# A list scheduler that orders the kernel: modulation weights may be loaded at any time, and dense products are drawn ahead of small ones when TensorE is counted as quiet

## The chip, the cores and the metric

One core of a Trainium2 chip runs the whole program. The metric is the time of one execution in device microseconds; less is better. Three runs of the kernel before took 2335.18, 2344.19 and 2348.64 us, so the median is 2344.19 us.

## What is computed

Two layers of a hybrid backbone over 512 latent and 256 context tokens, model width 1024. A layer is, cut to what matters here:

```python
sh_a, sc_a, gt_a, sh_m, sc_m, gt_m = ada_mod(cond, w_mod, b_mod)      # silu(cond) @ w_mod, 1024 x 6144
p = modulate(x, g_attn, sh_a, sc_a) @ w_in                            # one input projection
o_a = gdn_mixer(...)        # 8 heads of a gated delta rule, both directions, in chunks of 64 tokens
o_b = global_gqa(...)       # 4 query heads, all latent and context keys
o_c = window_gqa(...)       # 4 query heads, a band of keys and the context
x = x + gt_a * (concat(o_a, o_b, o_c) @ w_out)
x = x + gt_m * (square(relu(modulate(x, g_mlp, sh_m, sc_m) @ w1)) @ w2)
```

The context tokens go through the first layer in the same way. `ada_mod` depends on the conditioning alone, so its products can be made at any point before their results are used.

## The kernel before

**Work.** All products are split in a high and a low part and run as three passes. The input projection, the output projection and the MLP are dense: 128 rows by 128 columns of weights against 256 or 512 tokens. The delta rule is a chain over six pairs of token blocks ("units") and two groups of four heads: for each unit, `pre` builds and inverts the triangular blocks with many short operations of VectorE, GpSimd and 32x32 and 64x64 products, and `scan_step` carries the state forward with 64x64 and 128x64 products, whose PSUM tiles are called `pu`. The attention and all dense products use five PSUM banks called `ps`.

**Stages.** A layer has three phases. Phase 0 makes the input projection and the first group's chain, phase 1 the second group's chain, the attention and the modulation, phase 2 the output projection and the MLP. The program states the work in this order, but it isn't run in it.

**The order of the work.** `Program.layout` (L420) is a list scheduler that runs on the host while the kernel is built. It takes each operation's modelled duration from `cost` (L381), gives each a rank (the longest modelled path from it to the end of the program), and then steps through modelled time: on each of the four compute engines and on SyncE's queue, of the operations whose inputs are ready, the one with the highest rank goes next. The result is one fixed order of instructions for each engine. Nothing of it is decided on the chip, where each engine takes its instructions in that order and waits for its semaphores.

**Buffers.** A tile has a kind (L36 on) and takes one of that kind's slots when the first operation on it is placed (`room`, L494); an operation that finds no slot is set aside. Three kinds matter here. `sm` holds 512 KB of modulation weights and has two slots in phases 0 and 1. `st` holds the other weights, in three slots. `ps` is the PSUM kind, with five slots for everything dense.

**The modulation.** `mod_steps` makes a third `r` of the 6144 columns at a time: 16 loads of an `sm` tile, and from each tile four products of 32 rows by 256 columns, recorded as eight matmuls. All 64 products of one `r` add up in one `ps` tile, which is given back after the last of them. The first layer does `r` = 0 ahead of everything; `r` = 1, 2 and the next layer's `r` = 0 (48 loads) stand at the end of its phase 1. The second layer has `r` = 1 and 2 there (32 loads).

**The brake.** `AHEAD` (L50) and `HOARD` (L52) hold operations back (L545): an operation that needs a slot of a kind in `HOARD`, and whose rank is more than `AHEAD` of its engine behind the longest path still open, is laid aside until it comes within that distance. `AHEAD` is 1e5 ns for SyncE and practically endless for the others, so it is a brake on loads. `sm` is in `HOARD`, so the modulation loads are held back until 100 us of modelled path.

**TensorE's modelled clock.** The scheduler doubles a product's duration while it counts TensorE as cold. It keeps a sum of `dense` work in a running window; `dense` (`add`) is the share of the 128 rows that a product uses, times 0.6 if it has at most 64 columns. A modulation product, a weight product and a 128-row transpose count 1.0, the 64-row and 32-row products of the chain 0.15 to 0.5. The choice of the next operation does not look at that sum.

Of the kernel before, what the change touches and what calls it, by code (L numbers as in the profile page):

```python
# [48 lines left out]

AHEAD = (1e9, 1e9, 1e9, 1e9, 1e5)  # L50

HOARD = ("g", "sm", "t", "u", "a", "r", "kaq", "kv")  # L52

COPY = (0, 0, 0)
NU0 = 6
# [240 lines left out]
PE, ACT, DVE, POOL, SP = range(5)  # L296
# [3 lines left out]
WINDOW = 4096 / 1.2  # L300
COLD = 0.36
WARM = 0.66
TABLES = {AF.Exp: 0, AF.Tanh: 0, AF.Ln: 1}


class Program:
# [38 lines left out]
    def add(self, eng, name, args, kw):  # L345
# [30 lines left out]
        if eng == ACT:  # L376
            op.table = TABLES.get(args[2])
        self.ops.append(op)
# [41 lines left out]
    def layout(self):  # L420
        ops = self.ops
# [10 lines left out]
        for k, l in chains.items():  # L432
            n = KINDS[k][2] + KINDS[k][3] + max(KINDS[k][5:])
# [43 lines left out]
        clock, avail, future = [0.0] * 5, [[] for _ in range(5)], [[] for _ in range(5)]  # L477
        parked = {k: [] for k in KINDS}
        queues, front, order, table = 0.0, 0, [], 0
        warm, work, spill, window = False, 0.0, 0.0, 0  # L480
# [44 lines left out]
        while len(order) < len(ops):  # L525
            best = None
            for e in range(5):
                t = clock[e] if avail[e] else max(clock[e], future[e][0][0]) if future[e] else None
                if t is not None and (best is None or t < best[0]):
                    best = t, e  # L530
            if best is None and early:
                n = heapq.heappop(early)[1]
# [5 lines left out]
            t, e = best  # L538
            now = max(now, t)
            while future[e] and future[e][0][0] <= t:  # L540
                n = heapq.heappop(future[e])[1]
                heapq.heappush(avail[e], (-ops[n].rank, n))
            n = heapq.heappop(avail[e])[1]
            o = ops[n]
            if longest - o.rank > AHEAD[e] and n != front and n not in forced and any(  # L545
                    x.slot is None and x.kind in HOARD for x in o.tiles):
                heapq.heappush(early, (-o.rank, n))
# [10 lines left out]
            for x in o.tiles:  # L558
                if x.slot is None and x.kind in KINDS:
                    x.slot = got.pop(0)[1:]  # L560
                    r, i = x.slot
# [10 lines left out]
            if e == PE:  # L572

                w = int(t / WINDOW)
                while window < w:
                    warm = work > (COLD if warm else WARM) * WINDOW
                    work, window = spill, window + 1
# [3 lines left out]
                d = (end - t) * o.dense  # L581
                over = min(1.0, max(0.0, end - (w + 1) * WINDOW) / (end - t))
                work, spill = work + d * (1 - over), spill + d * over
# [16 lines left out]
            for x in o.tiles:  # L600
                if x.kind in KINDS:
                    x.left -= 1
                    x.end = max(x.end, end + 150)
                    if not x.left:
                        r, i = x.slot
# [14 lines left out]
            while early and (longest + early[0][0] <= AHEAD[ops[early[0][1]].eng] or early[0][1] == front):  # L620
                n = heapq.heappop(early)[1]
# [1161 lines left out]
```

## Time and profile before

| | |
|---|---|
| median of three runs | 2344.19 us |
| the profiled execution | 2342.02 us |
| its span | 2340.2 us |
| mean granted TensorE clock | 0.947 of full speed |
| matmul records on TensorE | 18792, busy 2143.4 us (92% of the span) |

The span is what the profiler's rows add up to; the execution's own time is 1.8 us longer. Times in rows are microseconds from the span's start. PE is TensorE (PEld its weight loads), DVE is VectorE, ACT is ScalarE, POOL is GpSimd, SPq is SyncE's queue, which issues all transfers. Nearly every instruction has the line L675, where the placed operations are issued, so rows are told apart by the names of the tiles: `ps<-sm,cs` is a modulation product, `ps<-b,w` a dense one, `pu<-...` one of the chain. Engines overlap, so busy times don't add up to the span.

### The profile page before, as it was taken

How to read it: one execution, taken by the hardware profiler on the slowest of the kernel's cores; microseconds unless marked ns; L12 is line 12 of the kernel's file. 1: busy time of each engine (PE TensorE's matmuls, PEld its weight loads, DVE VectorE, ACT ScalarE, POOL GpSimd, SP SyncE). 2: the span in 40 equal slices, each digit the busy share in tenths (PEclk: the TensorE clock that was granted, in tenths of full speed). 3: DMA queues.
4: the chain of work that ended last, by engine and by line, in shares of the span. 5: the costliest groups of instructions: out<-in, count | busy, mean ns of one | idle time of the engine just before them, and what ended most of it. 6: DMA issues, size and time to landing. Idle time of an engine off the chain costs nothing. (4 is left out here: it accounts for less than half of the span.)

```text
span 2340.2 us, 46868 instructions
## 1 busy us (share of the span) xinstructions
PE 2143.4 (92%) x18792; PEld 1688.3 (72%) x18792; DVE 1389.6 (59%) x3249; ACT 902.7 (39%) x1728; POOL 591.8 (25%) x1170
## 2 busy tenths in 40 slices
PE   5999998789978999999999898998769988999999
PEld 2787877456647788888888776688636666777777
DVE  4788677688764633333333487888876855334333
ACT  4756324455522521212122374543425544222321
POOL 0275435455440000000000025656763400000000
PEclk8999889799999999999999998999979989999999
DMA  7344323765453111221221224343574422223222
GB/s 277 96 133 123 108 83 96 220 177 166 143 160 116 53 57 64 70 72 46 73 72 59 95 80 121 96 134 110 155 208 138 151 73 84 87 90 105 94 90 81
DMA packets 170746, 260.63 MB, mean 111 GB/s; under 512 B 44448, under 2 KB 107424, under 8 KB 170528
## 3 DMA queue, kind: packets, MB, share of 16 engines
q1 hardware_dynamic: 170528, 257.64, 35.7%
q8 instruction: 147, 2.41, 0.4%
q14 instruction: 71, 0.58, 0.1%
HBM read 220.26 MB, written 37.32 MB: 110 GB/s over the span
## 5 line engine op out<-in xcount | busy, mean ns | idle before, releaser
L675 PE MATMUL ps<-b,w 128*128 128x512 f32 (+1 forms) x3936 | 848.1, 362 | 12.5 <-ACT b L675 6.7
L675 PEld LDWEIGHTS ps<-b,w 128*128 128x128 f32 x3936 | 655.4, 191 | 145.1 <-ACT b L675 10.1
L675 PE MATMUL ps<-h,w 128*128 128x512 f32 (+1 forms) x2304 | 480.8, 358 | 1.9 <-DVE w L675 0.9
L675 PEld LDWEIGHTS ps<-h,w 128*128 128x128 f32 x2304 | 381.6, 188 | 75.0 <-DVE w L675 4.9
L675 ACT ACTIVATE w<-st 128x1024 fp32r<-128x1024 f32 x192 | 197.9, 1054 | 572.9 <-PE ps L675 572.0
L675 DVE TENSOR_TENSOR w<-st,w 128x1024 fp32r<-128x1024 f32 x192 | 233.0, 1242 | 239.3 <-PE ps L675 163.1
L675 POOL TENSOR_TENSOR lb<-l,cst 128x72 fp32r<-128x72 f32 (+7 forms) x768 | 241.3, 350 | 62.4 <-ACT l L675 36.4
L675 DVE SCALAR_TENSOR_TENSOR x<-ps,mod,x 128x512 f32<-128x512 f32 (+1 forms) x120 | 77.2, 659 | 278.2 <-PE ps L675 278.0
L675 PE MATMUL ps<-w,b 128*128 128x256 f32 x1536 | 234.8, 298 | 4.8 <-DVE w L675 4.1
L675 ACT ACTIVATE g<-ps 128x512 f32<-128x512 f32 (+3 forms) x286 | 150.1, 540 | 199.4 <-PE ps L675 193.7
L675 PEld LDWEIGHTS ps<-w,b 128*128 128x128 f32 x1536 | 206.2, 197 | 14.4 <-DVE w L675 5.0
L675 POOL TENSOR_TENSOR g<-g 128x16 f32<-128x16 f32 x12 | 2.3, 225 | 720.5 <-ACT g L675 720.5
L675 DVE TENSOR_TENSOR q<-q,u 128x16 f32<-128x16 f32 (+4 forms) x360 | 131.3, 365 | 16.7 <-ACT u L675 10.6
L675 DVE TENSOR_TENSOR g<-g 128x512 f32<-128x512 f32 (+3 forms) x112 | 57.8, 541 | 120.6 <-ACT h L675 117.2
L675 ACT ACTIVATE u<-pu 128x384 f32<-128x384 f32 (+3 forms) x138 | 61.0, 449 | 150.1 <-PE pu L675 119.2
L675 DVE SCALAR_TENSOR_TENSOR g<-ps,par,g 128x511 f32<-128x511 f32 (+3 forms) x176 | 106.3, 618 | 7.8 <-ACT g L675 7.0
L675 PE MATMUL ps<-sm,cs 128*32 128x256 f32 x688 | 88.9, 445 | 19.5 <-DMA sm<-w_mod 14.0
L675 PE MATMUL ps<-cst,g 128*128 128x128 f32 (+1 forms) x502 | 90.3, 295 | 17.9 <-ACT g L675 11.3
L675 ACT ACTIVATE g<-ps,t 128x256 f32<-128x256 f32 (+2 forms) x144 | 75.3, 530 | 49.2 <-DVE t L675 41.8
L675 POOL TENSOR_TENSOR v<-u,gt 64x256 f32<-64x256 f32 x80 | 51.9, 649 | 148.0 <-DVE u L675 100.3
L675 PEld LDWEIGHTS ps<-cst,g 128*128 128x128 f32 (+1 forms) x502 | 59.3, 147 | 38.6 <-ACT g L675 21.6
L675 DVE TENSOR_TENSOR g<-g,g 128x512 f32<-128x512 f32 (+3 forms) x129 | 67.9, 546 | 29.1 <-ACT g L675 23.6
(138 smaller groups left out, 2665.8 us busy)
## 6 DMA issues: line engine op xcount, KB each, us to landing
st<-w SPq DMA_DIRECT2D x128, 512.0 KB, 4.3
sm<-w_mod SPq DMA_DIRECT2D x86, 512.0 KB, 4.7
st<-w_qkv SPq DMA_DIRECT2D x24, 512.0 KB, 4.4
st<-w_tm SPq DMA_DIRECT2D x24, 512.0 KB, 4.1
kv<-kv SPq DMA_DIRECT2D x96, 128.0 KB, 3.7
u<-gd SPq DMA_DIRECT2D x88, 128.0 KB, 3.5
kaq<-kq SPq DMA_DIRECT2D x80, 128.0 KB, 3.6
st<-w_out SPq DMA_DIRECT2D x16, 512.0 KB, 4.7
```

The lines of the kernel that those rows point to most:

```text
L675: getattr(engines[o.eng], o.name)(*[real(x) for x in o.args], **{k: real(x) for k, x in o.kw.items()})
```

## The change

`sm` leaves the list of kinds that are held back. And on TensorE, when the operation of highest rank is not dense (under 0.9), others are ready, and the modelled window has passed or its dense sum is behind (under half of the elapsed part while warm, under 0.8 of it while cold), then the ready dense operation of highest rank goes first, and the small one is put back.

```diff
-HOARD = ("g", "sm", "t", "u", "a", "r", "kaq", "kv")
+HOARD = ("g", "t", "u", "a", "r", "kaq", "kv")
...
+KEEP_WARM, GET_WARM, FULL = 0.5, 0.8, 0.9
...
             n = heapq.heappop(avail[e])[1]
+            if e == PE and ops[n].dense < FULL and avail[e]:
+
+                into = t - window * WINDOW
+                if t >= (window + 1) * WINDOW or work < (KEEP_WARM if warm else GET_WARM) * into:
+                    d = [x for x in avail[e] if ops[x[1]].dense >= FULL]
+                    if d:
+                        d = min(d)
+                        avail[e].remove(d)
+                        heapq.heapify(avail[e])
+                        heapq.heappush(avail[e], (-ops[n].rank, n))
+                        n = d[1]
             o = ops[n]
```

No operation is added, removed or resized. The instructions of each engine come in another order, and tiles take other slots.

## Rows read from the trace of the kernel before

**Rows 1.** The page's list of costly groups: TensorE's modulation products in the whole run.
```profile
L675 PE MATMUL ps<-sm,cs 128*32 128x256 f32 x688 | 88.9, 445 | 19.5 <-DMA sm<-w_mod 14.0 <-DVE cs L675 5.5
```

**Rows 2.** Windows by stage: length, busy us of each engine, PEclk, DMA share, GB/s.
```profile
60.00:240.00 180.00, 173.99 (x1589) 140.99 (x1589) 151.89 (x337) 115.34 (x186) 89.07 (x163) 1.00 0.42 120
240.00:400.00 160.00, 147.35 (x1783) 128.45 (x1784) 110.93 (x259) 56.56 (x111) 70.23 (x112) 0.90 0.29 87
400.00:500.00 100.00, 72.05 (x808) 44.43 (x808) 79.70 (x246) 37.73 (x105) 54.16 (x109) 0.74 0.76 218
500.00:640.00 140.00, 133.92 (x1918) 89.77 (x1919) 106.55 (x361) 77.85 (x222) 69.72 (x158) 0.98 0.48 147
640.00:712.00 72.00, 50.84 (x939) 32.33 (x938) 48.87 (x175) 19.30 (x47) 24.66 (x55) 0.87 0.48 147
...
1340.00:1640.00 300.00, 276.09 (x3161) 224.07 (x3160) 250.44 (x592) 155.90 (x265) 155.37 (x311) 0.94 0.38 107
1640.00:1760.00 120.00, 85.83 (x1228) 59.02 (x1227) 97.83 (x264) 34.90 (x78) 81.95 (x155) 0.83 0.64 182
1760.00:1880.00 120.00, 114.43 (x1680) 78.74 (x1680) 89.73 (x324) 65.29 (x185) 43.43 (x101) 0.97 0.43 134
```

**Rows 3.** The same stages, TensorE's modulation products alone: length, busy us, PEclk, DMA share.
```profile
400.00:500.00 100.00, 15.92 (x120) 0.74 0.76 218
500.00:640.00 140.00, 19.31 (x152) 0.98 0.48 147
640.00:712.00 72.00, 14.42 (x112) 0.87 0.48 147
...
1640.00:1760.00 120.00, 15.57 (x112) 0.83 0.64 182
1760.00:1880.00 120.00, 17.64 (x144) 0.97 0.43 134
```

**Rows 4.** Timeline of TensorE at the end of the first layer's phase 1.
```profile
659.03 0.65 PE L675 MATMUL pu<-s,u 32*32 32x32 f32 x32 [3.03 <-POOL s L675]
...
707.60 1.09 PE L675 MATMUL pu<-cst,u 128*128 128x128 f32 x4 [7.48 <-DVE u L675]
709.90 15.30 PE L675 MATMUL ps<-b,w 128*128 128x512 f32 x64 [1.21 <-ACT b L675]
```

**Rows 5.** Timeline of SyncE's queue: first modulation loads of phase 1, and a late run of them.
```profile
408.05 0.82 SPq L675 DMA_DIRECT2D sm<-w_mod  x2
...
662.70 23.92 SPq L675 DMA_DIRECT2D sm<-w_mod  x7
```

**Rows 6.** The chain that ended last, between 1735 and 1770 us.
```profile
1739.90 5.85 DMA sm<-w_mod
...
1747.93 6.24 DMA a<-kB
```

**Rows 7.** Windows of 20 us, all instructions, columns as in Rows 2.
```profile
240.00:260.00 20.00, 15.53 (x257) 10.84 (x258) 14.58 (x32) 10.99 (x20) 11.12 (x27) 0.74 0.15 50
...
320.00:340.00 20.00, 18.16 (x173) 14.94 (x171) 11.87 (x24) 6.09 (x14) 5.01 (x5) 0.80 0.45 137
340.00:360.00 20.00, 20.00 (x153) 18.63 (x153) 12.39 (x40) 5.12 (x10) 13.89 (x32) 0.83 0.30 87
1420.00:1440.00 20.00, 16.94 (x271) 14.54 (x270) 16.49 (x33) 5.81 (x12) 11.28 (x30) 0.82 0.37 111
1440.00:1460.00 20.00, 18.24 (x157) 14.29 (x158) 14.45 (x40) 5.19 (x10) 8.89 (x16) 0.83 0.27 76
```

**Rows 8.** Two of these windows, TensorE's products with weights alone, columns as in Rows 3.
```profile
240.00:260.00 20.00, 5.73 (x24) 0.74 0.15 50
...
340.00:360.00 20.00, 17.96 (x113) 0.83 0.30 87
```

**Rows 9.** Waits of the whole run: TensorE for VectorE to read out a bank.
```profile
PE ps L675 <- DVE g L675: 17.6, 9, 4.2
```

**Rows 10.** Window of 20 us in the first layer's input projection, columns as in Rows 2.
```profile
120.00:140.00 20.00, 20.00 (x162) 17.14 (x162) 15.41 (x27) 11.32 (x19) 11.05 (x21) 1.00 0.83 242
```

## The prediction

> **What bounds the kernel now.** I read first what the edit can touch, the modulation products: 688 records, 88.9 us of TensorE in the run [rows 1]. The table of stages then says where TensorE is short of time and where it isn't [rows 2]. Phase 0 of the first layer (60 to 400 us) keeps it busy for 321.3 of 340 us. Then come 400 to 500 us with 72.05 of 100, 500 to 640 with 133.92 of 140, and the end of phase 1, 640 to 712, with 50.84 of 72. The second layer repeats this: 276.09 of 300 us, then 85.83 of 120, then 114.43 of 120. So in each layer TensorE is full, then starved, then full again, and the first layer ends starved. The same stages with the modulation products alone show what the brake does: none before 400 us, 15.92 us in the starved stage, 19.31 us in the full one, 14.42 us at the end; in the second layer 15.57 and then 17.64 us in the full stage [rows 3]. The first of these loads after the opening goes out at 408 us [rows 5], though nothing but the brake keeps it from 60 us on. The timeline of the first layer's end shows small products waiting 3.03 us for GpSimd and 7.48 us for VectorE: there the delta-rule chain sets the end, and the modulation fills holes [rows 4]. The chain of waits has one more place: a modulation load of 5.85 us, and right behind it the attention's keys, 6.24 us [rows 6].
>
> **The brake off, first layer.** Nothing is added; work moves. The 48 loads may go from 60 us on, and their products have the lowest rank, so they run where the plan sees TensorE free or where the new rule prefers them.
>
> (a) The 19.31 us in the full stage 500 to 640 leave it. TensorE is 96% busy there, so I count all of it: -19.3 us (bounds 0, if the chain sets the pace there too, and -19.3).
>
> (b) The 14.42 us at the end leave too. TensorE is free for 21.2 of 72 us, so the cover is the chain's latency: -2 us (bounds 0 and -14.4).
>
> (c) Those 33.7 us go ahead of 500 us. TensorE is free there for 6.0 + 12.7 + 28.0 = 46.6 us [rows 2], but in holes of a few us, and the plan fills only holes that it foresees; a product put in a full stretch pushes what is behind it. Bounds 0 and +33.7; between them no row decides, so I take half, +16.9.
>
> Sum of the first layer: -4.4 us.
>
> **The brake off, second layer.** (d) 17.64 us leave 1760 to 1880, where TensorE is 95% busy: -17.6 us (bounds 0 and -17.6). (e) They go ahead of 1760, where 23.9 + 34.2 = 58.1 us are free, more than three times as much; again half, +8.8 (bounds 0 and +17.6). (f) The load in the chain of waits is gone from its place by then: -6 us, the 5.85 of that landing (bounds 0, and -12.1 if the keys behind it also land at once). Sum: -14.8 us.
>
> What queues behind what: SyncE issues in one order. Earlier, an `sm` load waits there for the products that read its slot before; behind it stand weight loads, stores of keys and queries, and the units' inputs, for which TensorE and GpSimd wait. In a late stretch seven such loads took 23.92 us of the queue's time [rows 5]. I count nothing for this, since the plan puts a load only after the slot's modelled end; the price, if that cover is gone, is a rival below.
>
> The stretch 120 to 140 us has the transfers at 0.83 and 242 GB/s [rows 10], so a load of 512 KB there costs the weight load behind it about 512 KB / 242 GB/s = 2.2 us. The Trainium skill says (DMA: Bandwidth & Descriptors, section "Issuing engines are not separate DMA queues") that all transfers of a core end on the same 16 engines and interleave there, which speaks against moving loads into that stretch; by it ten loads in the 40 us around it would cost up to 22 us, where TensorE has no slack. I take 0, since TensorE is full there and the slots of `sm` come free slowly.
>
> **Dense ahead of small.** (g) Gain. The granted clock is 0.90 over 240 to 400 and 0.94 over 1340 to 1640 [rows 2]; full speed throughout would give back 0.10 x 160 + 0.06 x 300 = 34 us, the bound on one side, with 0 on the other. But 340 to 360 us lies at 0.83 with 17.96 of 20 us in weight products [rows 7, 8]: dense work was already there. In 240 to 260 (clock 0.74, weights only 5.73 us), 320 to 340 (0.80), 1420 to 1440 (0.82) and 1440 to 1460 (0.83) there is something to mix; these lost 5.2 + 4.0 + 3.6 + 3.4 = 16.2 us. I take half, -8. The starved stages have lower clocks still (0.74 and 0.83), but what TensorE lacks there is ready work, and the modulation that filled them is partly spent earlier, so I count no gain from them.
>
> (h) Cost. Each swap makes a small product of the chain, and all behind it in the queue, wait for a dense one: 15.30 us / 64 = 0.24 us by the run of 128x512 products [rows 4]. The trace doesn't show how many swaps there are. If they fill half of the time at the low clock (2 x 34 = 68 us) and all of it lies on the chain, they cost 34 us; if dense work is ready anyway and the order merely changes, nothing. TensorE is full in those stages, so the order there costs little: +4.
>
> **Sum.** -4.4 - 14.8 - 8 + 4 = -23.2 us against the profiled execution's 2342.0, so 2318.8. The median lies 2.2 us above that execution, so I forecast 2321 us, with a range of its own of 2304 to 2332.
>
> **Rivals.** *All holes absorb.* If (c) and (e) are 0, because enough foreseen holes lie ahead, the sum is -19.3 - 2 - 17.6 - 6 - 8 + 4 = -49, or 2295 us. For it: 105 us are free ahead of the full stages for 51 us of work. Against: the holes of phase 0 are short. Chance 0.15.
>
> *The work moves and nothing ends sooner.* If the plan sees no holes that the chip has, (c) is +33.7 and (e) +17.6: -19.3 - 2 + 33.7 - 17.6 + 17.6 - 6 - 8 + 4 = +2, so about 2346 us. For it: phase 0 is full, and the first layer's end is the chain's, not TensorE's. This is also the case in which the change doesn't do what it says, as when the loads go early and their products keep their rank's late place. Chance 0.23.
>
> *A bank is missing (slower).* All 64 products of one third add up in one of the five `ps` banks. Started early and fed drop by drop, that third holds a bank through most of phase 0, where the projection's slices need banks while VectorE reads them out. The nearest price: nine waits of TensorE for VectorE's read-out sum to 17.6 us, so 1.96 us each, with five banks [rows 9]. If each of the 24 slices of the two layers waits so once more, that is +47, and with -23 the time is 2368 us. It decides from (23 + 12) / 24 = 1.5 us for each slice. Against it: the attention, in the full stages, then has that bank back. Chance 0.14. The Trainium skill (Perfetto Trace Analysis, section "Matmul Optimizations") asks that all PSUM banks be used, and a bank parked for a sum in waiting goes against it; the trace so far bears it out only with nine short waits.
>
> *SyncE's queue is held (slower).* If seven early loads hold the queue as the late ones did, 23.92 us each layer, units and weights come late: +48 - 23 = +25, or 2369 us. Against it: in that late stretch little else had to be issued. Chance 0.08.
>
> **How the numbers follow.** Forecast 0.40. Half a per cent, 11.7 us, is about what a measurement of this kernel can tell from no change (its three runs span 13.5 us). Faster by more: 0.40 + 0.15 = 0.55. Same: 0.23. Slower: 0.14 + 0.08 = 0.22. Both signs have weight, so the range reaches beyond the forecast's own: down to 2285, which holds the absorbed case with 10 us below it, and up to 2362, which holds the unmoved case and the smaller half of the slower ones. Left out are some 0.05 below and 0.13 above.
>
> **What would show it.** Right: modulation products from 60 to 400 us and from 1340 to 1640, few or none after 500 and 1760; the stages 500 to 640 and 1760 to 1880 shorter by 15 us or more; attention loads no longer behind modulation loads; a clock above 0.90 and 0.94 in phase 0. Wrong: the attention starting later by as much as its stage is shorter (the moved work was pushed, not absorbed); TensorE waiting for VectorE or ScalarE before `ps` products in phase 0 (the bank); SyncE waiting for `ps` products ahead of weight loads (the queue); or a longer stretch of small products in the starved stages, with a lower clock, since their filler is gone.

## The result, and the profile after

The changed kernel takes 2369.9 us (median of four runs, 2360.5 to 2371.7), beside 2342.6 us for the kernel before in the same session: a ratio of 1.011, 95% interval 1.007 to 1.015. It is slower by 27 us, where 2321 us and a gain were forecast, and above the range. The profiled execution took 2370.42 us, with a span of 2368.6 us.

Before the stages, the span is best split in two: the time in which TensorE was busy, and the rest. The page's list of engines, after:

```profile
PE 2183.9 (92%) x18792; PEld 1713.3 (72%) x18792; DVE 1390.9 (59%) x3249; ACT 904.1 (38%) x1728; POOL 600.4 (25%) x1170
```

Busy time of PE rose from 2143.4 to 2183.9 us, by 40.5 us, for the same 18792 products. The rest of the span fell from 2340.2 - 2143.4 = 196.8 to 184.7 us, by 12.1. The difference of the spans, 28.4 us, is +40.5 - 12.1: TensorE doesn't wait longer, its products take longer. The mean clock is the same, 0.947 in both. By the trace's record of the clock, TensorE was busy at the lower level (1.2 GHz) for 184.8 us before and 198.8 us after; if busy time there counts half, that is an estimated 7 us of the 40.5, and 33.5 us are left.

The windows up to the first layer's residual sum, and from there to the second layer's, before (columns as in [rows 2]):

```profile
0.00:722.90 722.90, 623.04 (x7272) 459.65 (x7273) 532.69 (x1447) 339.24 (x728) 308.18 (x601) 0.91 0.49 150
722.90:1929.90 1207.00, 1123.53 (x9853) 917.11 (x9852) 692.57 (x1607) 445.13 (x848) 283.63 (x569) 0.95 0.32 96
```

and after:

```profile
0.00:749.60 749.60, 639.94 (x7287) 474.02 (x7288) 535.38 (x1447) 338.24 (x727) 303.58 (x601) 0.91 0.47 145
749.60:1956.90 1207.30, 1145.73 (x9839) 926.76 (x9839) 691.40 (x1607) 447.58 (x849) 296.78 (x569) 0.96 0.31 95
```

The first part is longer by 26.7 us (PE busy +16.9, idle +9.8), the second by 0.3 (busy +22.2, idle -21.9). In both TensorE does about the same products in more time.

The stages of [rows 2], after. A stage here covers other work than before, since everything comes later:

```profile
60.00:240.00 180.00, 168.06 (x1536) 130.53 (x1536) 134.01 (x291) 105.54 (x171) 80.81 (x161) 0.99 0.50 144
240.00:400.00 160.00, 149.24 (x1678) 128.84 (x1676) 118.78 (x281) 58.27 (x105) 68.94 (x110) 0.98 0.31 95
400.00:500.00 100.00, 75.59 (x979) 50.05 (x979) 77.39 (x233) 39.30 (x101) 49.35 (x98) 0.80 0.69 200
500.00:640.00 140.00, 128.72 (x1677) 88.60 (x1676) 108.23 (x356) 71.17 (x201) 68.58 (x139) 0.94 0.49 149
640.00:712.00 72.00, 56.60 (x1039) 41.84 (x1039) 53.44 (x194) 26.45 (x79) 32.68 (x84) 0.82 0.16 49
```

Between 240 and 400 us the granted clock is 0.98, against 0.90 before: most of the low-clock time of [rows 7] is gone. TensorE was busy 1.9 us longer there and made 1678 products against 1783. The counts alone say little, since these are other products: by shape, 818 of 128x128 against 751, but 276 of 64x64 against 360 and 512 of 32x32 against 576. The same work in more time shows only in the whole run.

The modulation products alone, after (columns as in [rows 3]):

```profile
60.00:240.00 180.00, 7.21 (x88) 0.99 0.50 144
240.00:400.00 160.00, 2.48 (x8) 0.98 0.31 95
400.00:500.00 100.00, 16.15 (x128) 0.80 0.69 200
500.00:640.00 140.00, 18.08 (x129) 0.94 0.49 149
640.00:712.00 72.00, 0.00 (x0) 0.82 0.16 49
...
1340.00:1640.00 300.00, 1.68 (x16) 0.95 0.38 109
1640.00:1760.00 120.00, 16.65 (x104) 0.89 0.61 181
1760.00:1880.00 120.00, 20.07 (x128) 0.88 0.45 141
```

The full stages kept them: 18.08 us against 19.31, and 20.07 against 17.64. What went early (9.7 us before 400) came out of the first layer's end, where 14.42 us became none.

What TensorE does with its time is in its timeline. In the changed kernel, where 64 products `pu<-s,s` of 32x32 are next in the chain and dense `ps<-w,b` are ready:

```profile
261.78 0.31 PE L688 MATMUL pu<-s,s 32*32 32x32 f32 x10
262.01 0.38 PE L688 MATMUL ps<-w,b 128*128 128x256 f32 x1
262.33 0.32 PE L688 MATMUL pu<-s,s 32*32 32x32 f32 x12
262.57 0.38 PE L688 MATMUL ps<-w,b 128*128 128x256 f32 x1
262.88 0.31 PE L688 MATMUL pu<-s,s 32*32 32x32 f32 x10
263.12 0.38 PE L688 MATMUL ps<-w,b 128*128 128x256 f32 x1
263.43 0.31 PE L688 MATMUL pu<-s,s 32*32 32x32 f32 x12
263.68 0.50 PE L688 MATMUL ps<-w,b 128*128 128x256 f32 x2
264.11 0.38 PE L688 MATMUL pu<-s,s 32*32 32x32 f32 x20
264.42 1.56 PE L688 MATMUL ps<-w,b 128*128 128x256 f32 x11
```

The rule of the change has broken one run of small products into five, with one or two dense products in each gap. From the first start to 264.42 that is 2.64 us for 64 small and 5 dense products. The same kinds in unbroken runs, in the timeline of the experiment e5_runs:

```profile
287.12 4.30 PE L685 MATMUL ps<-w,b 128*128 128x256 f32 x34
291.35 0.75 PE L685 MATMUL pu<-s,s 32*32 32x32 f32 x64
292.03 2.85 PE L685 MATMUL ps<-w,b 128*128 128x256 f32 x22
```

Here 64 small ones take 0.68 us (291.35 to 292.03), and a dense one 4.23 / 34 = 0.124 us. That makes 0.68 + 5 x 0.124 = 1.30 us. The broken order costs 1.34 us more, for eight more changes between the two shapes: 0.17 us each. The granted clock is 1.00 in both stretches, and TensorE is busy all the time, so no list of waits shows it.

### The profile page after: what moved, and what is told of

Same layout as the page of the kernel before. It is cut to its first block, busy times and chain, and to the rows that moved or that the text cites. A ratio compares the mean times of both kernels' runs of the same rounds, so it can differ in the third digit from the quotient of the medians.

```text
span 2368.6 us, 46878 instructions
## 1 busy us (share of the span) xinstructions
PE 2183.9 (92%) x18792; PEld 1713.3 (72%) x18792; DVE 1390.9 (59%) x3249; ACT 904.1 (38%) x1728; POOL 600.4 (25%) x1170
## 4 chain that ended last, share of the span: by engine, by line
PE 66%; DVE 10%; POOL 2%; issue 2%; ACT 2%; DMA 1%; SPq 0%; ACTq 0%; DVEq 0%; POOLq 0%
PE ps L688 58%; PE pu L688 8%; DVE q L688 3%; DVE t L688 2%; DVE g L688 1%; POOL lb L688 1%; DVE u L688 1%; ACT g L688 1%; DVE w L688 1%; DVE kaq L688 0%; POOL g L688 0%; DMA sm<-w_mod 0%; DVE v L688 0%; ACT w L688 0%; ACT u L688 0%
## 5 line engine op out<-in xcount | busy, mean ns | idle before, releaser
L688 POOL TENSOR_TENSOR lb<-l,cst 128x72 fp32r<-128x72 f32 (+7 forms) x768 | 246.2, 355 | 85.7 <-ACT l L688 47.9
L688 PE MATMUL ps<-w,b 128*128 128x256 f32 x1536 | 241.4, 297 | 4.1 <-DVE w L688 3.5
L688 ACT ACTIVATE g<-ps 128x512 f32<-128x512 f32 (+4 forms) x286 | 149.9, 540 | 215.3 <-PE ps L688 212.5
L688 DVE TENSOR_TENSOR q<-q,u 128x16 f32<-128x16 f32 (+4 forms) x360 | 141.5, 393 | 16.0 <-ACT u L688 10.0
L688 PE MATMUL ps<-sm,cs 128*32 128x256 f32 x688 | 94.4, 452 | 21.7 <-DMA sm<-w_mod 16.0
L688 DVE SCALAR_TENSOR_TENSOR g<-ps,par,g 128x510 f32<-128x510 f32 (+3 forms) x176 | 106.2, 617 | 7.4 <-ACT g L688 6.6
L688 ACT ACTIVATE u<-pu 64x256 f32<-64x256 f32 (+3 forms) x138 | 61.3, 449 | 125.5 <-PE pu L688 99.5
L688 PE MATMUL pu<-u,kaq 64*64 64x64 f32 (+1 forms) x1344 | 84.1, 241 | 5.7 <-DVE u L688 4.1
```

The source lines that it names most:

```text
L688: getattr(engines[o.eng], o.name)(*[real(x) for x in o.args], **{k: real(x) for k, x in o.kw.items()})
```

## The experiments

Four theories were set against each other. **A:** the early modulation products push the rest, and the first layer's end lacks its filler. **B:** a dense product drawn ahead delays the chain. **C:** any new order differs by some 10 us or more, whatever made it. **D:** each time TensorE leaves small products for dense ones and comes back costs it about 0.23 us (0.20 to 0.235 by the starts of neighbouring products without idle time between them), and the change adds round trips. The expectation of e4_unbroken counts some 106 of them; the schedulers' orders have 431 runs of small products before and 526 after, which is 95 more, and in the traces the runs of products that use fewer than 128 rows number 415 and 504. Where an expectation gives the runs of a kernel not yet on the chip, they are counted in the order that its scheduler wrote.

A finer count was made once all had run, and it stands in the table: how often the part of the array that a product uses (the first figure in the timeline's rows, 32\*32, 64\*64, 128\*64, 128\*128 ...) is another than that of the product before it. Busy time and the rest of the span are those of the profiled execution, which is not the median: in e10 and e12 it took 2381.1 and 2325.3 us, 11 and 12 us more.

| kernel | changes of shape | PE busy, us | span less busy | median, us | ratio (95%) |
|---|---|---|---|---|---|
| before | 1172 | 2143.4 | 196.8 | 2342.6 | |
| after | 1372 | 2183.9 | 184.7 | 2369.9 | 1.011 (1.007-1.015) |
| e1_loads_only | 1166 | 2155.0 | 219.2 | 2377.6 | 1.016 (1.013-1.019) |
| e2_mix_only | 1417 | 2198.6 | 195.3 | 2399.8 | 1.025 (1.022-1.029) |
| e3_placebo | 1190 | 2145.0 | 201.6 | 2348.1 | 1.004 (1.002-1.005) |
| e4_unbroken | 1184 | 2139.5 | 189.6 | 2335.8 | 1.000 (0.997-1.003) |
| e5_runs | 1004 | 2098.3 | 203.6 | 2304.4 | 0.987 (0.984-0.989) |
| e6_many_runs | 2806 | 2683.5 | 215.8 | 2901.0 | one run |
| e7_runs_loads | 1013 | 2110.1 | 187.9 | 2296.5 | 0.982 (0.980-0.985) |
| e8_loads_placebo | 1190 | 2157.0 | 185.6 | 2341.1 | 1.001 (0.999-1.003) |
| e9_both | 998 | 2096.6 | 206.7 | 2304.1 | 0.986 (0.984-0.988) |
| e10_after_placebo | 1347 | 2186.0 | 193.1 | 2370.4 | 1.013 (1.010-1.017) |
| e11_mix_placebo | 1376 | 2182.0 | 184.4 | 2368.6 | 1.012 (1.008-1.015) |
| e12_best_placebo | 1022 | 2116.8 | 206.7 | 2313.2 | 0.989 (0.986-0.993) |

Each ratio is to runs of the kernel before beside it on the same chip (their medians lie between 2337.2 and 2342.6 us).

### Each half alone, and neither

**e1_loads_only:** only `sm` is taken off the brake.

```diff
-HOARD = ("g", "sm", "t", "u", "a", "r", "kaq", "kv")
+HOARD = ("g", "t", "u", "a", "r", "kaq", "kv")
```

> The brake on the modulation loads is taken off, the choice of dense products is left as before. Theory A (the early products push a full TensorE, and the end of the first layer's phase 1 runs at the low clock for want of filler): this part alone makes nearly all of the change, 2360 to 2372 us, with the first scan output of the first layer 8 to 15 us later than before (174 us) and a granted clock under 0.7 in the last 50 us of phase 1. Theory B (the swaps of dense ahead of small products delay the chain): 2335 to 2350 us, the loss is in the other part. Theory C (the order is reshuffled and any order differs by some 10 us): no relation to the parts; the gains and losses of the two parts don't add up to the whole.

**e2_mix_only:** only the rule that draws dense products ahead, as in the change; `sm` stays on the brake.

> Dense products are drawn ahead of small ones, the modulation loads stay held back. Theory A: 2330 to 2348 us, no loss; the end of the first layer's phase 1 keeps its modulation products and a granted clock over 0.85. Theory B: 2360 to 2372 us, with the scan outputs of the first layer later by 15 us or more. Theory C: anything between 2325 and 2365.

**e3_placebo:** neither; GpSimd's modelled cost is 2 ns higher, which alone shuffles the order.

```diff
-            return 148 + (1.667 if op.name != "tensor_tensor" or n < 400 else 2.0) * n, 0
+            return 150 + (1.667 if op.name != "tensor_tensor" or n < 400 else 2.0) * n, 0
```

> Neither part: the kernel before, with the scheduler's modelled cost of a GpSimd operation raised from 148 to 150 ns, which changes the order in places that have nothing to do with the change. Theories A and B: within 10 us of the kernel before. Theory C: as far away as the change, 15 us or more in either direction.

Both halves lost, by 1.6 and 2.5%, and each more than the two together; the shuffle lost 0.4%. So the parts don't add up, and a loss of e1's size had to be tried in another order before it could be blamed on the loads (e8). Neither theory A nor B had these times: 2377.6 us lies above A's range for e1, and 2399.8 above all ranges for e2. The shuffle is smaller than theory C wanted (15 us). The two lose in different places. e2 has TensorE busy for 55 us more. e1 has 11.6 us more of that and 22.4 us more of the rest: it stands still in the second layer, where the chain of waits of e1_loads_only reads

```profile
1724.62 4.38 DMA qC<-r
...
1737.11 4.00 DMA sm<-w_mod
1741.16 1.12 PE ps L675 x8
1742.72 4.59 DMA kC<-r
...
1750.24 5.95 DMA a<-kB
```

The collision of [rows 6], a modulation load and then the attention's keys, is still there, with the stores of queries and keys around it.

### The change without its broken runs

**e4_unbroken:** the changed kernel, but a dense product is drawn ahead only where the product before it was dense. The rule may put off a run; it can't break into one.

```diff
...
-            if e == PE and ops[n].dense < FULL and avail[e]:
+            if e == PE and ops[n].dense < FULL and avail[e] and full:
...
+                full = o.dense >= FULL
```

> The changed kernel, but a dense product is drawn ahead of a small one only where the product before was dense too, so a run of small products is never broken; the order then has 419 runs of small products in place of 526. Theory D (each change from dense to small products and back costs TensorE about 0.23 us, read from the starts of neighbouring products, and the change made some 106 more such round trips): the loss of the change goes, 2335 to 2352 us, and TensorE's busy time falls from 2184 to about 2160 us. Theory B (a dense product drawn ahead delays the chain, wherever it is drawn): 2360 us or more, since the drawing stays. Theory C (the order is reshuffled, and any order differs by some 10 us): anything from 2330 to 2375.

One condition takes away the whole loss: 2335.8 us, PE busy 2139.5 us, 1184 changes of shape. The loads and a part of the drawing ahead are still in it (the rule now acts in fewer places), so neither loses by being there at all.

### Fewer runs than before, and many more

**e5_runs:** the kernel before, with the opposite rule: after a small product, a ready small one goes ahead of a dense one of higher rank.

```diff
...
+            if e == PE and not full and ops[n].dense >= FULL:
+                d = [x for x in avail[e] if ops[x[1]].dense < FULL]
+                if d:
+                    d = min(d)
...
+                full = o.dense >= FULL
```

> The kernel before with neither part of the change and one rule of the opposite kind: after a small product, a ready small product goes ahead of a dense one of higher rank, so runs of small products grow; 323 runs in place of 431. Theory D: 108 fewer round trips at 0.23 us, some 25 us less than before where TensorE is full, 2315 to 2330 us, TensorE's busy time near 2120 us. Theory B: the chain is served earlier too, so 2325 to 2345. Theory C: 2330 to 2360.

**e6_many_runs:** only the drawing rule, with both shares at 0.9 in place of 0.5 and 0.8, so that it acts nearly everywhere.

> The second part of the change alone, as in the run with mixing only, with both thresholds at 0.9, so that dense products are drawn nearly always: 1237 runs of small products in place of 533. Theory D: 806 more round trips than before at 0.23 us, TensorE's busy time up by some 185 us to about 2330 us, and a time of 2480 to 2540 us. Theory B: the chain is delayed by the drawing, but TensorE's busy time stays within 40 us of 2199. Theory C: within 30 us of the run with mixing only, 2400 us.

e5 is 1.35% faster than the kernel before, with busy time 45.1 us lower and 168 fewer changes. e6 takes 2901 us: 1634 more changes, 540 us more of busy time. Both lie beyond what theory D expected (2315 to 2330 and 2480 to 2540 us): its direction is right, its price was too low. The timeline of e6 shows the cost by itself:

```profile
200.20 0.50 PE L688 MATMUL ps<-b,w 128*128 128x512 f32 x1
200.63 0.24 PE L688 MATMUL pu<-s,s 32*32 32x32 f32 x2
200.80 0.50 PE L688 MATMUL ps<-b,w 128*128 128x512 f32 x1
```

One dense and two small products take 0.60 us, from 200.20 to 200.80. The dense one takes 0.24 us by the run of 64 in [rows 4] (a little high, since that run begins at a clock of 0.63), and two of 64 that take 0.68 us come to 0.02. So two changes cost 0.34 us, 0.17 each, as in the changed kernel; the granted clock is 1.00 here too. But e6's loss is larger than that, 0.33 us for each change. Its mean clock is 0.837, and the same group, a few us later at the lower level, takes 0.96 us, from 205.19 to 206.15:

```profile
205.19 0.80 PE L688 MATMUL ps<-b,w 128*128 128x512 f32 x1
205.91 0.31 PE L688 MATMUL pu<-s,s 32*32 32x32 f32 x2
206.15 0.69 PE L688 MATMUL pu<-lb,bdb 128*128 128x384 f32 x1
```

TensorE of e6 is busy at that level for 800.4 us, against 184.8 before. With such time counted half, an estimated 232 of the 540 us are left, 0.14 us for each change.

### The loads again, with and without runs

**e7_runs_loads:** e5_runs and `sm` off the brake. **e8_loads_placebo:** e1_loads_only and the 2 ns of e3_placebo. **e9_both:** e4_unbroken and the rule of e5_runs.

> The kernel before with the rule that continues a run of small products (as in e5_runs) and with the modulation slots no longer braked. If the time is set by the number of changes between small and dense products on TensorE (theory D), the plan's 311 runs of small products against 323 in e5_runs leave it at 2295 to 2315 us, beside 2304 of e5_runs, and TensorE's busy time near 2098 us. If taking off the brake costs its 38 us by itself (e1_loads_only), as loads that push attention's work aside, it comes out at 2335 to 2350 us.

> e1_loads_only with GpSimd's planned cost per operation changed by 2 ns, as in e3_placebo: the same unbraked slots, another order from chance alone. If the loads themselves cost what e1_loads_only lost, it stays at 2365 to 2385 us. If that loss was the meeting of particular transfers in that one order (theory C), it comes out 15 us or more away from 2377 us, between 2335 and 2360 us. By theory D alone, 437 runs of small products against the 431 of before give 2340 to 2350 us.

> The change with both mends: dense products are drawn ahead only where the product before was dense (e4_unbroken), and a run of small products is continued (e5_runs). By theory D the plan's 303 runs of small products give 2295 to 2310 us, the lowest time of all, with TensorE's busy time at 2090 to 2100 us. By theory B (dense products drawn ahead delay the chain, broken run or not) it is 15 us or more above e5_runs: over 2319 us.

e8 takes 2341.1 us: the loss of e1 came with its order, not with the loads alone. Two windows of e1_loads_only in the second layer's starved stage

```profile
1720.00:1740.00 20.00, 10.32 (x62) 5.62 (x62) 3.35 (x7) 5.09 (x10) 0.00 (x0) 0.67 0.40 114
1740.00:1760.00 20.00, 10.92 (x122) 4.96 (x124) 8.71 (x31) 2.36 (x5) 4.43 (x5) 0.59 0.95 273
```

and the same of e8_loads_placebo

```profile
1720.00:1740.00 20.00, 17.05 (x194) 9.80 (x190) 9.11 (x25) 5.05 (x12) 16.28 (x39) 0.66 0.57 175
1740.00:1760.00 20.00, 11.36 (x262) 6.71 (x262) 15.30 (x44) 4.24 (x9) 12.06 (x23) 0.76 0.98 288
```

show the standstill gone: TensorE is idle for 11.6 of the 40 us against 18.8, and makes 456 products against 184. But e8's equal time hides two opposite changes. Its parts, split as before at the residual sums:

```profile
0.00:745.80 745.80, 640.80 (x7287) 474.69 (x7288) 543.54 (x1448) 337.55 (x725) 304.29 (x601) 0.88 0.47 146
745.80:1932.20 1186.40, 1119.30 (x9838) 915.78 (x9837) 683.16 (x1607) 443.69 (x847) 295.06 (x569) 0.96 0.32 97
```

The first is 22.9 us longer than in the kernel before, at a clock of 0.88 instead of 0.91, and the second 20.6 us shorter. e7 is the fastest of all at 2296.5 us, 1.8% under the kernel before, so the loads cost nothing in sum there; and e9 equals e5. Dense products are still drawn ahead in e9, and it loses nothing. That weakens theory B without refuting it, since the rule acts in fewer places there, and no trace shows in how many. What speaks against B as the main cause is the split of the span: a chain that is delayed would show as waiting, and the changed kernel waits 12.1 us less.

### The verdicts in a second order

**e10_after_placebo**, **e11_mix_placebo** and **e12_best_placebo** are the changed kernel, e2_mix_only and e7_runs_loads with the 2 ns of e3_placebo.

> The changed kernel with GpSimd's planned cost per operation changed by 2 ns, as in e8_loads_placebo: its two rules in another order. The plan has 510 runs of small products, 79 more than before. By theory D they cost 79 times 0.23, so 2350 to 2370 us, and TensorE's busy time is about 2165 to 2185 us against 2143. If the loss of the change was one order's bad luck (theory C), it comes out between 2330 and 2347 us, though the runs stay broken.

> e2_mix_only with the same 2 ns: only the drawing of dense products, in another order; 528 runs in the plan, 97 more than before. By theory D alone 2350 to 2372 us. e2_mix_only had 2400 us, some 30 more than its runs explain: if that rest was luck of the order, it is gone here; if dense products drawn ahead also delay the attention itself when the weights are braked, this one too is over 2385 us.

> e7_runs_loads with the same 2 ns; 308 runs in the plan. If the gain of e7_runs_loads comes from its fewer runs (theory D), it stays at 2290 to 2315 us with TensorE busy for 2095 to 2115 us; if it was luck of the order (theory C), it is over 2325 us.

The loss of the change comes back in another order (2370.4 us), and the drawing rule alone gives about the same, 2368.6. e2's further 31 us were its order's. The gain of e7 shrinks by 16.7 us to 1.1% and stays clear of no change. The five pairs that differ by those 2 ns lie, by their ratios, 6, 9, 17, 33 and 36 us apart. That is how little a single order proves here, and theory C is right to that extent, but busy time sorts itself by the changes of shape throughout. A straight line through the thirteen kernels without e6 rises by 0.22 us for each change, no kernel is more than 13 us off it, and the correlation is 0.98. The 200 changes that were added make 0.22 x 200 = 44 us by it, and 40.5 us were measured. A part of that slope is the clock: with busy time at the lower level counted half, it is 0.17 us for each change, no kernel is more than 8 us off, and the change's 33.5 us come to 0.17 us as well. That is an estimate, but it agrees with the two timelines.

## Why the prediction was wrong

**(h) is the step that failed**, by its mechanism. I priced a swap as a small product waiting 0.24 us behind a dense one, saw that TensorE was full there, and wrote that "the order there costs little: +4". What costs is not the wait but the change of shape on TensorE itself, and a full TensorE is just where nothing hides it. The term was +40.5 us of busy time, 0.17 us for each change in two timelines and 0.22 over the runs. My upper bound of 34 us was counted on the wrong thing, and that it came near is luck. e4 (one condition less, no loss), e5 (the opposite rule, a gain) and e10 and e11 (the loss in other orders) show it.

The Trainium skill (TensorEngine Tiling (Array Packing), section "Tiling Modes", under "Key Properties") has the rule that I missed: changing the tiling mode, and not only the tile, drains TensorE. It gives no price there. The trace agrees that a change costs, at 0.17 us; that the time goes into draining, no run here shows. A change of shape also parts a product from others of its kind, and no run tells these two apart.

**(a) and (d), -19.3 and -17.6, didn't happen.** The full stages kept 18.08 and 20.07 us of modulation. I let the loads go early and took the products to follow, but these keep the lowest rank, and wherever phase 0 has other work they come last.

**(b) was right, and its cover held.** The 14.42 us left the end of the first layer. The last attention product ends at 653 us before and 676 after, the output projection starts at 709.9 and 733.2: 56 and 57 us. The chain sets that stretch, as said, though its filler is gone and its clock lower (0.58 between those two times, against 0.85 before). So the second half of theory A costs little. Early loads can cost the first layer more than that: up to the first residual sum of e8, TensorE is busy at the lower level for 134 us, against 95 before and 98 in the changed kernel. Why e8 pays there and the changed kernel doesn't stays open.

**(c) and (e), +16.9 and +8.8:** ahead of 500 us there are 25.8 us of modulation against 15.92, and ahead of 1760 us 18.3 against 15.57. Little moved, so there was little to push. Taken together the loads are worth nothing that stands out from the 6 to 36 us by which orders differ: e8 equals the kernel before, e7 is 8 us under e5 and e12 9 us over it, and the changed kernel and e10, with early loads, lie within 2 us of e11, which holds them back. The sum of (a) to (f), -19 us, was work that stayed where it was.

**(f), -6 us, is not settled.** The changed kernel doesn't have the collision in its chain of waits between 1730 and 1860 us (a modulation load of 3.73 us stands there at 1855.94, with no keys behind it), and its second layer has 21.9 us less idle time. But e1 has the collision with the brake off, and e10 has 16 us of that idle time back. The order decides it, and a brake is no remedy.

**(g), -8 us: the clock rose as predicted, but not by the swaps, and they gave nothing.** Phase 0 of the first layer, before and after, in the windows of either trace:

```profile
60.00:400.00 340.00, 321.33 (x3370) 269.44 (x3369) 262.82 (x595) 171.90 (x296) 159.30 (x275) 0.95 0.36 104
```

```profile
60.00:400.00 340.00, 317.30 (x3212) 259.37 (x3211) 252.79 (x571) 163.81 (x276) 149.75 (x270) 0.98 0.41 121
```

The clock went from 0.95 to 0.98. The window holds 96 modulation products more and 254 others fewer, so its count proves no loss by itself. But the rise isn't the swap's: with the loads alone this window is at 0.97 and 0.98 (e1, e8), with as many modulation products (101 and 108), 1586 and 1585 products of 128x128 and 960 of 32x32, where the changed kernel has 1524 and 896. The drawing rule added no clock to that and left less done. It raised the changes of shape in the window from 223 to 266, and the scheduler's model has no term for them.

**The rivals.** *The work moves and nothing ends sooner* (2346 us) describes what the loads did, and e8 (2341 us) is its time. The two slower rivals gave about the measured time, 2368 and 2369, for reasons that weren't at work. *The bank:* TensorE's waits for VectorE's read-out are shorter than in [rows 9]:

```profile
PE ps L688 <- DVE g L688: 14.4, 8, 3.5
```

*SyncE's queue* was indeed held, longer than in [rows 5]:

```profile
42.36 30.36 SPq L688 DMA_DIRECT2D sm<-w_mod  x8
```

Yet TensorE was busy for 56.70 us of 40 to 100, against 55.13 before, and between 40 and 200 us it waited 1.3 us for transfers in all: what stood behind those loads was not needed yet. A rival on the mechanism that decided was missing, though [rows 4] had both ingredients: small products and dense ones, in the one place where the trace keeps them apart.

## What to carry to other kernels

On a full TensorE, keep products of one shape together: here each change of shape cost about 0.17 us, and 0.22 us with the clock that fell beside it, more than a 128x256 product (0.124 us), so filling single dense products into a run of small ones loses even where the clock is full. When a reordering makes a busy engine busier with the same instructions, no list of waits shows the cost; compare busy time with the count, and look at the timeline for short groups. And repeat such an experiment in a second, nearly equal order before a part of it is blamed or praised.

## What was not expected of the hardware

A TensorE that never rests can be granted the lower clock. In e6_many_runs, where single dense products alternate with pairs of 32x32 ones:

```profile
200.00:220.00 20.00, 20.00 (x87) 11.46 (x87) 4.86 (x15) 5.33 (x8) 4.79 (x10) 0.61 0.12 35
```

and in the kernel before:

```profile
200.00:220.00 20.00, 20.00 (x306) 14.72 (x293) 16.35 (x34) 13.13 (x23) 11.98 (x27) 1.00 0.32 83
```

Both are busy for 20.00 of 20 us. The one at 0.61 of full speed (mostly at 1.2 GHz) did 87 products, the one at 1.00 did 306. Of 128x128 alone, the counts are 35 and 56. So a rule that draws dense products ahead nearly always, to keep the clock, ended with a mean clock of 0.837 against 0.947. The busy share of these rows counts the time of a change as work; what the clock goes by, they don't show.
